# Sums of MLP weights: where GpSimd begins their transfers, and in what pieces

## The chip, the core and the metric

The kernel runs on one core of a Trainium2 chip. The core has a matrix engine (TensorE, PE in the profile, with its weight loads as PEld), a vector engine (VectorE, DVE), a scalar engine (ScalarE, ACT), a general engine (GpSimd, POOL) and a queue engine that only issues transfers (SyncE, SP). Sixteen DMA engines carry all transfers. Each engine takes its instructions in the order in which they were written into the program, and semaphores make it wait for the others. The metric is the device time of one execution in microseconds (us).

## The reference, cut to what matters

Two layers of a transformer run over 1024 latent tokens and 256 context tokens of width 1024, in 32-bit floats. Each layer computes a modulation from a conditioning vector, one input projection whose columns feed three mixers (latent attention, differential attention, a chunk mixer), an output projection, and a gated MLP with a convolution of three taps along the tokens.

```python
def conv_ffn(h, p):
    u = dwconv3(h @ p["ffn_wup"], p["ffn_convw"], p["ffn_convb"])
    gate, val = jnp.split(u, 2, axis=-1)
    return (jax.nn.silu(gate) * val) @ p["ffn_wdown"]

def layer(x, xc, mod, modc, rows, cols, p, layer_idx, need_ctx):
    sh1, sc1, g1, sh2, sc2, g2 = jnp.split(mod, 6, axis=-1)
    csh1, csc1, cg1, csh2, csc2, cg2 = jnp.split(modc, 6, axis=-1)
    y, yc = mixer(x * (1.0 + sc1) + sh1, xc * (1.0 + csc1) + csh1, rows, cols, p, layer_idx, need_ctx)
    x = layer_norm(DN_ALPHA * x + g1 * y, p["ln1_g"], p["ln1_b"])
    x = layer_norm(DN_ALPHA * x + g2 * conv_ffn(x * (1.0 + sc2) + sh2, p), p["ln2_g"], p["ln2_b"])
    ...
    return x, xc
```

The weights `ffn_wup` (1024 x 5632) and `ffn_wdown` (2816 x 1024) of each layer are what the change is about. The context tokens pass through the MLP in layer 0 only.

## The kernel before, in words

**The sums.** The two products of the MLP are computed with a scheme of Strassen's kind: a matrix is cut into two by two blocks, and seven block products replace eight. The scheme needs sums of weight blocks, such as block (1,0) plus block (1,1). The kernel has these sums made in DRAM by transfers alone: one transfer copies a block of weights into a scratch tensor, and a second one adds another block onto it on its way (an accumulation). The up weights of a layer have four such sums, kept in the tensor `ws`, and the down weights four more, kept in `db`. Two of the four are made from the inputs alone, the other two add a sum that is already made. All of these transfers are begun by POOL, in the function `sums` (the copy in line 592, the accumulation in line 593), and each sum is cut into chunks of 1408 KB: four chunks for a sum in `ws` and two for one in `db`. That makes 32 transfers for `ws` and 16 for `db` in each layer, 96 in all. `SUMROWS` and the function `flat` set the shape of a chunk: 176 rows of 2048 numbers, so 8 KB a row. A copy may join rows, and goes as 32 rows of 45 KB; an accumulation keeps rows of 8 KB.

**Where they are begun.** `sums` returns a list of steps, and `begin_sums(n)` takes the next n of them. Before the change the list for `ws` of layer 0 is made at the very start. In the input projection of each layer (`in_chunk`) one step is taken at every fourth tile. What is left is spread over the attention, between the pieces of the modulation, as fill (`program`). In the first part of the MLP (`ffn`, the "up" part) a new list is made, the `db` of this layer and, in layer 0, the `ws` of layer 1, and one or two steps are taken for each of 22 blocks of columns; what is left of it is begun in layer 1's input projection and attention.

**The order of the work.** The program is not written out in its final order. Each step is a task with the engines that may do it, an estimate of its time on each, the tasks that it depends on and a key. A planner (`Sched.run`) goes through time with these estimates and gives each engine the ready task with the smallest key, inside a window of 450 tasks. A sum's transfer is a task of 1.0 us on POOL with 120 added to its key and 40 us of delay after it, whatever its shape. The order that comes out is fixed: on the chip each engine follows its own list. So a step that takes longer than planned delays all that stands behind it on its engine.

**What else POOL does.** In the attention POOL joins the two maps of differential scores (lines 1237 and 1238, some 4.3 us for 1280 keys), which PE transposes one block of queries later (line 1262), and takes the low parts of weights (line 457). A block is one head and 256 queries, so layer 0 has 20 blocks and layer 1 has 16. In the MLP POOL makes combinations of blocks (line 1490).

**The readers of the sums.** `up_load` reads `ws`, and `down_load` reads `db`, both through SP; `sum_chunks` names the chunks that a read has to wait for. The MLP's up part stores its result in `da` (and `dc` for the context), from which the down part reads it again. Line 1671 is the scalar part of the convolution, and line 1650 the vector instruction that frees PE's accumulator for the next block. The input projection stores some of its results in `zd` (line 444 issues every transfer of SP).

Of the kernel before, what the change touches and what calls it, by code (L numbers as in the profile page):

```python
# [15 lines left out]
ALU = mybir.AluOpType  # L16
# [4 lines left out]
P = 128  # L21
# [9 lines left out]
NF = FF // P  # L31
NP = NF // 2
# [34 lines left out]
SIZES = [1280] * 17 + [1536] * 8 + [2560] * 8  # L67
LARGE = 512
UNIT = 64
SUMROWS = 176  # L70
SLACK = 150
AHEAD = 300

# [317 lines left out]
class Kern:  # L391
# [120 lines left out]
    def center(self, x, sums):  # L512

        nc = self.nc
        nm, ss, sq = self.st(), self.st(), self.C()
        self.task(dve_t(1), lambda e: nc.vector.tensor_scalar(nm.t, sums[0].t, sums[1].t, -1.0 / D, op0=ALU.add, op1=ALU.mult), sums, [nm])

        self.task(act_t(D, 0.19), lambda e: nc.scalar.activation(sq.t.bitcast(BF16), x[:, :D], AF.Square, bias=nm.t, accum_out=ss.t), [x, nm], [sq, ss])
        return nm, self.rsqrt1(lambda: ss.t, 1.0 / D, EPS, [ss])

    def norm(self, x, sums):

        nm, y = self.center(x, sums)
        b = self.st()
        self.task(dve_t(1), lambda e: self.nc.vector.tensor_tensor(out=b.t, in0=nm.t, in1=y.t, op=ALU.mult), [nm, y], [b])
        self.task(act_t(D, 0.18), lambda e: self.nc.scalar.activation(x[:, :D], x[:, :D], AF.Identity, scale=y.t, bias=b.t), [x, y, b], [x])
# [49 lines left out]

    def flat(self, x, c):

        return x.rearrange("n p c -> (n p c)").rearrange("(r c) -> r c", c=2048)[c * SUMROWS:(c + 1) * SUMROWS]

    def sums(self, l, which):

        src = self.i["wup" if which == "ws" else "w_down"]
        x = (self.ws if which == "ws" else self.db)[l]
        w = lambda a, b: (lambda: src[l, a, b])
        out = []

        def make(n, c, a, b, r=()):
            key = (which, l, n, c)
            put = lambda: self.flat(x[n], c)  # L590
            kw = dict(w=[key], key=MODKEY, late=40.0)
            out.append(lambda: self.s.add({"pool": 1.0}, lambda e: self.nc.gpsimd.dma_start(out=put(), in_=self.flat(a(), c)), (), **kw))
            out.append(lambda: self.s.add({"pool": 1.0}, lambda e: self.nc.gpsimd.dma_start(out=put(), in_=self.flat(b(), c), accum_op=ALU.add, max_dma_last_dim=8192), [*r, key], **kw))

        for c in range((NF if which == "ws" else NP) * P * 512 // (SUMROWS * 2048)):
            at = lambda n: (which, l, n, c)
            if which == "ws":
                make(0, c, w(1, 0), w(1, 1))
                make(2, c, w(1, 0), w(0, 0))
                make(1, c, w(0, 0), lambda: x[0], [at(0)])  # L600
                make(3, c, w(0, 1), lambda: x[1], [at(1)])
            else:
                make(0, c, w(0, 0), w(0, 1))
                make(1, c, w(0, 1), w(1, 1))
                make(2, c, w(1, 1), lambda: x[0], [at(0)])
                make(3, c, w(1, 0), lambda: x[2], [at(2)])
        return out
# [6 lines left out]

    def sum_chunks(self, name, l, n, f):
        a, b = f * P * 512, (f + 1) * P * 512 - 1
        m = SUMROWS * 2048
        return [(name, l, n, c) for c in range(a // m, b // m + 1)]


# [260 lines left out]
    def in_chunk(self, l, name, tabs):  # L881
        i = self.i
        if (l, name) not in self.inw:
            self.chunk_weights(l, name)
        wk, wb = self.inw.pop((l, name))
        if name == "dk":
            tabs["d"] = td = self.C(F32, (P, 8, 2, 32))
            self.dma(lambda: td.t, lambda: i["dtab"], 4 * P * 512, w=[td])
        elif name == "kv":
            tabs["k"] = tk = self.S(F32, (P, 8, 2, 64))  # L890
            self.dma(lambda: tk.t, lambda: i["ktab"], 4 * P * 1024, w=[tk])
            self.kvT = [(self.S(F32R), self.S(F32R)) for _ in range(2)]
            self.krs = self.S(F32R)
        elif name == "q":
            self.qlT = {p: (self.S(F32R, (P, 3, 256)), self.S(F32R, (P, 3, 256))) for p in range(NT // 2)}
        held = []
        tiles = range(0 if l == 0 or name in ("kv", "dk", "dv") else 2, NT)
        if name == "z":
            tiles = (8, 9, 0, 1) if l == 0 else (6, 7, 8, 9, 2, 3, 4, 5)
        for n, t in enumerate(tiles):  # L900
            if name != "z" and n % 4 == 1:
                self.begin_sums(1)
            r = self.in_tile(l, name, t, wk, wb, tabs)
            if r is not None:
                held.append(r)
                if len(held) == 2:
                    self.transpose_lat(name, t - 1, held)
                    held = []
# [881 lines left out]
    def ffn(self, l):  # L1790
        nc, i = self.nc, self.i
# [3 lines left out]
        self.dn_raw, self.dn_ops = [], []  # L1795
        order = self.up_order(l)
        last = order[-1][1]
        assert not self.due
        self.due = self.sums(l, "db") + (self.sums(1, "ws") if l == 0 else [])
        done = 0  # L1800
        for x in order:
            if len(x) == 2:
                self.emit_rest(x)
                continue
            done += x[2] != 1
            self.up_operands(l, done - 1 + UP_LOOK)
            f = x[0]
            self.up_slot(l, *x)
            if f >= 2 and (x[1] == "22" or l == 0 and f % 2 and x[1] == "S2"):
                self.begin_sums(1)  # L1810
            if f == NF - 1 and x[1] == "S3":
                self.down_load(l, 2)
            if f == NF - 1 and x[1] == "22":
                self.down_prep(l, 1)
            if x[1] == last and f % 2:
                self.store_pair(l, f // 2, self.blocks[f - 1:f + 1])
                self.blocks[f - 1] = self.blocks[f] = None
# [5 lines left out]
        for n, pr in enumerate(DOWN):  # L1823
# [14 lines left out]
            if n in (2, 4):  # L1838
                for t, u in pairs:
                    x = u if n == 2 else t  # L1840
# [10 lines left out]
            for m, (t, u) in enumerate(pairs):  # L1851
# [3 lines left out]
                a, b = acc[t], acc[u]  # L1855
# [49 lines left out]
    def program(self):  # L1905
        self.setup()
        self.first_hT()
        self.due = self.sums(0, "ws")
        for l in range(DEPTH):
            self.in_proj(l)  # L1910
            self.att_setup(l)
            ada = [(0, n) for n in range(8, 24)] + [(1, n) for n in range(8)] if l == 0 else [(1, n) for n in range(8, 24)]
            ada = [lambda a=a: self.mod_piece(*a, MODKEY) for a in ada]
            m, d = len(ada), len(self.due)
            fill = []
            for j, a in enumerate(ada):
                fill += [lambda: self.begin_sums(1)] * ((j + 1) * d // m - j * d // m) + [a]
            self.attention(l, fill)
            self.out_tiles(l, NT, True)
            self.ffn(l)  # L1920
# [103 lines left out]
```

## Time and profile before

| what | value |
|---|---|
| runs shown, median (lowest to highest) | 3523.48 us (3515.53 to 3527.67) |
| the profiled execution's own time | 3522.21 us |
| its span, first to last instruction | 3520.4 us |
| PE busy, share of the span | 3210.6 us, 91% |
| DVE busy | 2586.0 us, 73% |
| ACT busy | 1652.2 us, 47% |
| POOL busy | 1045.3 us, 30% |
| DMA queue of SP, share of 16 engines | 34.1% (386.22 MB) |
| DMA queue of POOL, share of 16 engines | 15.9% (138.42 MB) |

The span is 1.8 us shorter than the execution's own time. In the program's order the first layer's input projection lies at about 130 to 345 us, its attention at 345 to 870, the up part of its MLP from about 980 to 1665 and the down part to 2080; the second layer's input projection lies at 2080 to 2180, its attention at 2180 to 2670, its up part at about 2800 to 3265 and the down part to the end. A share over the whole span mixes these stages, so the prediction reads each of them by itself. "Issue" as a releaser means that the profile shows nothing that the engine waited for.

### The profile page before, as it was taken

To read this page: it belongs to the slowest core of one execution; us is meant where nothing else is said; L and a number is where in the kernel's file an instruction comes from. 1 tells how busy PE (TensorE), PEld (TensorE's weight loads), DVE (VectorE), ACT (ScalarE), POOL (GpSimd) and SP (SyncE) were. 2 spreads that over 40 slices of the span, in tenths; PEclk is the share of its full clock that TensorE was granted. 3 is DMA by queue.
4 is the path that set the end of the run, shared out by engine and by line. 5 is a ranking of instruction groups with operands and counts; after the bars stand their busy time and mean duration, and the time that the engine had idled before them with its cause. 6 is when DMAs were issued, how large, how long until landed. Compare 5 with 4: busy or idle time off the path is not lost. (4 is left out here: it accounts for less than half of the span.)

```text
span 3520.4 us, 53639 instructions
## 1 busy us (share of the span) xinstructions
PE 3210.6 (91%) x18953; PEld 2801.2 (80%) x18953; DVE 2586.0 (73%) x6262; ACT 1652.2 (47%) x2931; POOL 1045.3 (30%) x678
## 2 busy tenths in 40 slices
PE   7799999998988889989998899999998889999997
PEld 5798888787977777777886799888888867788775
DVE  7456988988777566657569737889898776666687
ACT  5024666565344344434435404566663445454543
POOL 3101555553122111213034301454434232212143
PEclk9899999999999999999999999999998999999998
DMA  8823444443345666664765743132313556653672
GB/s 324 206 65 100 116 120 131 120 106 104 111 145 168 191 176 181 191 173 147 225 217 188 213 130 78 49 77 82 89 53 121 163 157 200 201 163 132 222 263 102
DMA packets 274839, 528.07 MB, mean 150 GB/s; under 512 B 67465, under 2 KB 119177, under 8 KB 264585
## 3 DMA queue, kind: packets, MB, share of 16 engines
q1 hardware_dynamic: 263048, 386.22, 34.1%
q0 software_dynamic: 11520, 138.42, 15.9%
q8 instruction: 149, 2.44, 0.3%
q14 instruction: 122, 0.99, 0.1%
HBM read 444.25 MB, written 218.69 MB: 188 GB/s over the span
## 5 line engine op out<-in xcount | busy, mean ns | idle before, releaser
L447 PE MATMUL t<-region 128*128 128x256 f32 (+4 forms) x15631 | 2876.0, 342 | 233.4 <-DVE region L457 69.7
L447 PEld LDWEIGHTS t<-region 128*128 128x128 f32 x15631 | 2458.0, 194 | 584.9 <-DVE region L457 82.6
L457 DVE TENSOR_TENSOR region<-region 128x512 fp32r<-128x512 f32 (+6 forms) x867 | 765.2, 907 | 267.8 <-ACT region L460 225.0
L460 ACT ACTIVATE region<-t 128x512 fp32r<-128x512 f32 (+4 forms) x935 | 452.6, 511 | 717.1 <-PE t L447 326.0
L460 ACT ACTIVATE region<-region 128x512 fp32r<-128x512 f32 (+4 forms) x944 | 591.2, 662 | 384.8 <-PE t L447 131.9
L457 POOL TENSOR_TENSOR region<-region 128x512 fp32r<-128x512 f32 (+5 forms) x289 | 403.9, 1408 | 1123.2 <-ACT region L460 804.6
L1490 POOL TENSOR_TENSOR region<-region 128x512 f32<-128x512 f32 (+2 forms) x107 | 212.0, 1984 | 911.3 <-ACT region L460 355.2
L1673 DVE SCALAR_TENSOR_TENSOR region<-region,conv 128x1023 f32<-128x1023 f32 x176 | 233.4, 1327 | 165.6 <-ACT region L1671 165.3
L1198 ACT ACTIVATE region<-region,q 128x1280 f32<-128x1280 f32 (+1 forms) x216 | 273.5, 1267 | 165.2 <-DVE q L1197 148.7
L1193 DVE TENSOR_SCALAR_CACHE_REDUCE region<-t 128x512 f32<-128x512 f32 (+1 forms) x600 | 333.6, 586 | 9.4 <-PE t L447 8.0
L457 DVE TENSOR_TENSOR region<-t,region 128x512 fp32r<-128x512 f32 (+1 forms) x529 | 297.8, 598 | 46.4 <-ACT region L460 41.6
L1262 PE MATMUL t<-ident,region 128*128 128x128 f32 x1312 | 186.1, 285 | 19.9 <-DVE region L1193 5.0
L1238 POOL TENSOR_TENSOR region<-region 128x1280 f32<-128x1280 f32 (+1 forms) x69 | 188.4, 2731 | 5.8
L1262 PEld LDWEIGHTS t<-ident,region 128*128 128x128 f32 x1312 | 154.9, 147 | 27.6 <-DVE region L1193 8.2
L1671 ACT ACTIVATE region<-region,conv 128x1024 f32<-128x1024 f32 x88 | 109.2, 1241 | 128.2 <-DVE region L1654 56.7
L1237 POOL TENSOR_SCALAR region<-region,q 128x1280 f32<-128x1280 f32 (+1 forms) x69 | 87.4, 1267 | 205.6 <-DVE q L1232 128.2
L447 PE MATMUL t<-region,s 128*4 128x256 f32 x768 | 118.2, 291 | 17.2 <-ACT region L460 10.8
L1490 DVE TENSOR_TENSOR region<-region 128x512 f32<-128x512 f32 (+2 forms) x150 | 113.3, 760 | 18.4 <-POOL region L1490 15.3
L1018 DVE TENSOR_TENSOR region<-t,region 128x256 f32<-128x256 f32 x32 | 13.6, 424 | 126.5 <-PE t L447 69.6
L447 PEld LDWEIGHTS t<-region,s 128*4 128x4 f32 x768 | 64.8, 87 | 46.4 <-ACT region L460 11.3
L548 POOL TENSOR_TENSOR region<-region 128x1024 f32<-128x1024 f32 x26 | 72.8, 2815 | 93.3 <-DMA region<-n 65.6
L1688 ACT ACTIVATE region<-region 128x1024 f32<-128x1024 f32 x66 | 53.4, 839 | 63.9 <-DVE region L1673 63.9
(137 smaller groups left out, 1849.5 us busy)
## 6 DMA issues: line engine op xcount, KB each, us to landing
ws<-in_wup POOLq DMA_DIRECT2D x48, 1408.0 KB, 9.8
region<-ws SPq DMA_DIRECT2D x176, 256.0 KB, 3.7
region<-in_ada_w SPq DMA_DIRECT2D x160, 256.0 KB, 3.5
region<-in_wup SPq DMA_DIRECT2D x154, 256.0 KB, 3.0
da<-region SPq DMA_DIRECT2D x154, 256.0 KB, 3.7
region<-da SPq DMA_DIRECT2D x154, 256.0 KB, 4.0
db<-in_w_down POOLq DMA_DIRECT2D x24, 1408.0 KB, 8.5
ws<-ws POOLq DMA_DIRECT2D x16, 1408.0 KB, 14.3
```

What stands on the lines that cost most here:

```text
L447: self.nc.tensor.matmul(ps, a, b, start=start, stop=stop, skip_group_check=again)
L457: eng.tensor_tensor(out=out, in0=full, in1=hi.bitcast(F32), op=ALU.subtract)
L460: self.nc.scalar.activation(out, in_, AF.Copy, **kw)
L548: self.task(engs or pool_t(D), lambda e, row=row, op=op: self.vec[e].tensor_tensor(out=x[:, :D], in0=x[:, :D], in1=row.t, op=op), [x, row] ...
L1193: self.task(dve_t(b - a), lambda e: nc.vector.tensor_scalar(p[:, a:b], ps[:, :b - a], -scale, None, op0=ALU.mult, op1=ALU.min, accum_out=n ...
L1198: self.task(act_t(nk, 0.19), lambda e: nc.scalar.activation(p[:, :nk], p[:, :nk], AF.Exp, bias=m.t, scale=-1.0, accum_out=s.t), [p, m], [p ...
L1237: nc.gpsimd.tensor_scalar(p2[:, :nk], p2[:, :nk], cc.t, 0.0, op0=ALU.mult, op1=ALU.add)
L1238: nc.gpsimd.tensor_tensor(out=p1[:, :nk], in0=p1[:, :nk], in1=p2[:, :nk], op=ALU.add)
L1262: nc.tensor.transpose(ps[:, u, j * P:(j + 1) * P], B[key][j][:, (kt + u) * P:(kt + u + 1) * P], self.ident)
L1490: self.task(either(n), lambda e: self.vec[e].tensor_tensor(out=o(), in0=a(), in1=b(), op=op), r, w, **kw)
L1671: self.task(act_t(n, 0.15), lambda e: nc.scalar.activation(t.t, u(0, n), AF.Identity, scale=c[:, 1:2], bias=c[:, 3:4]), r + ["conv"], [t])
L1673: self.task(dve_t(n - 1, extra=0.06), lambda e, d=d: nc.vector.scalar_tensor_tensor(t[:, 1 - d:n - d], u(d, n - 1 + d), c[:, 2 * d:2 * d + ...
```

## The change

All 48 transfers of a layer's sums are now taken as fill in the attention of that layer, spread evenly between the pieces of its modulation. Neither the input projection nor the MLP begins any. The rows of a chunk become 704 rows of 512 numbers, 2 KB a row, for copies and accumulations alike; a chunk still has 1408 KB and there are still 96 transfers. The space in which POOL keeps what it has put out for the DMA engines (`dynamic_dma_scratch_size`) grows from 1024 to 2048 bytes.

```diff
-SUMROWS = 176
+SUMROWS = 704
...
     def flat(self, x, c):
-        return x.rearrange("n p c -> (n p c)").rearrange("(r c) -> r c", c=2048)[c * SUMROWS:(c + 1) * SUMROWS]
+        return x.rearrange("n p c -> (n p) c")[c * SUMROWS:(c + 1) * SUMROWS]
...
-            out.append(lambda: self.s.add({"pool": 1.0}, lambda e: self.nc.gpsimd.dma_start(out=put(), in_=self.flat(a(), c)), (), **kw))
-            out.append(lambda: self.s.add({"pool": 1.0}, lambda e: self.nc.gpsimd.dma_start(out=put(), in_=self.flat(b(), c), accum_op=ALU.add, max_dma_last_dim=8192), [*r, key], **kw))
+            out.append(lambda: self.s.add({"pool": 1.0}, lambda e: self.nc.gpsimd.dma_start(out=put(), in_=self.flat(a(), c), max_dma_last_dim=2048), (), **kw))
+            out.append(lambda: self.s.add({"pool": 1.0}, lambda e: self.nc.gpsimd.dma_start(out=put(), in_=self.flat(b(), c), accum_op=ALU.add, max_dma_last_dim=2048), [*r, key], **kw))
...
-        for n, t in enumerate(tiles):
-            if name != "z" and n % 4 == 1:
-                self.begin_sums(1)
+        for t in tiles:
...
-        assert not self.due
-        self.due = self.sums(l, "db") + (self.sums(1, "ws") if l == 0 else [])
...
-            if f >= 2 and (x[1] == "22" or l == 0 and f % 2 and x[1] == "S2"):
-                self.begin_sums(1)
...
-        self.due = self.sums(0, "ws")
         for l in range(DEPTH):
             self.in_proj(l)
             self.att_setup(l)
...
+            self.due = self.sums(l, "ws") + self.sums(l, "db")
             m, d = len(ada), len(self.due)
...
-    nc = _bacc.Bacc("TRN2", target_bir_lowering=False, num_devices=1, dynamic_dma_scratch_size=1024)
+    nc = _bacc.Bacc("TRN2", target_bir_lowering=False, num_devices=1, dynamic_dma_scratch_size=2048)
```

The planner places the rest anew, so the order changes on every engine. From line 900 on the changed program's line numbers are smaller by two, and from line 1800 on by up to six. The places on which the prediction rests are on POOL. The first is POOL's list in the first input projection, before the change; a row with `x2` stands for two equal instructions, and 176x2048 is the shape of an accumulation:

```order
L592 DMA ws<-in_wup 32x11264
L593 DMA ws<-in_wup 176x2048 x2
L948 TENSOR_TENSOR region<-region 128x256
L593 DMA ws<-in_wup 176x2048
L457 TENSOR_TENSOR region<-region 128x1280
L1027 TENSOR_TENSOR region<-region 128x256
L593 DMA ws<-in_wup 176x2048
L593 DMA ws<-ws 176x2048 x2
L592 DMA ws<-in_wup 32x11264
L593 DMA ws<-ws 176x2048
L457 TENSOR_TENSOR region<-region 128x1152
L593 DMA ws<-ws 176x2048
```

The same place in the changed program, with the first transfers at its end:

```order
L457 TENSOR_TENSOR region<-region 128x1280
L457 TENSOR_TENSOR region<-region 128x768
L937 TENSOR_TENSOR region<-region 128x256 x2
L946 TENSOR_TENSOR region<-region 128x256
L457 TENSOR_TENSOR region<-region 128x1280
L1025 TENSOR_TENSOR region<-region 128x256
L457 TENSOR_TENSOR region<-region 128x1152
L592 DMA ws<-in_wup 704x512 x2
L457 TENSOR_TENSOR region<-region 128x2x2x32
L457 TENSOR_TENSOR region<-region 128x256
```

The ten copies and accumulations of the first list have gone from among the tiles of the projection, and the first sums begin behind its last weight (128x1152).

The second place is in the attention of the first layer, about two thirds through it. Before, one transfer stands between several blocks' joins (L1237, L1238):

```order
L457 TENSOR_TENSOR region<-region 128x512 x6
L1237 TENSOR_SCALAR region<-region,q 128x1280
L1238 TENSOR_TENSOR region<-region 128x1280
L1237 TENSOR_SCALAR region<-region,q 128x1280
L1238 TENSOR_TENSOR region<-region 128x1280
L593 DMA ws<-in_wup 176x2048
L457 TENSOR_TENSOR region<-region 128x512 x3
L1237 TENSOR_SCALAR region<-region,q 128x1280
L1238 TENSOR_TENSOR region<-region 128x1280
L1237 TENSOR_SCALAR region<-region,q 128x1280
L1238 TENSOR_TENSOR region<-region 128x1280
L592 DMA ws<-in_wup 32x11264
```

In the changed program (where the joins are L1235 and L1236):

```order
L1235 TENSOR_SCALAR region<-region,q 128x1280
L1236 TENSOR_TENSOR region<-region 128x1280
L1235 TENSOR_SCALAR region<-region,q 128x1280
L1236 TENSOR_TENSOR region<-region 128x1280
L593 DMA ws<-ws 704x512
L593 DMA ws<-in_wup 704x512 x2
L457 TENSOR_TENSOR region<-region 128x10x64
L592 DMA ws<-in_wup 704x512
L457 TENSOR_TENSOR region<-region 128x512
L592 DMA db<-in_w_down 704x512
L457 TENSOR_TENSOR region<-region 128x512 x2
```

Five transfers of 704 rows stand there with two small steps between them.

The third place is the up part of the first layer's MLP, before:

```order
L1490 TENSOR_TENSOR region<-region 128x512 x3
L593 DMA db<-db 176x2048
L1490 TENSOR_TENSOR region<-region 128x1024
L592 DMA db<-in_w_down 32x11264
L593 DMA db<-in_w_down 176x2048
L1490 TENSOR_TENSOR region<-region 128x1024
L1490 TENSOR_TENSOR region<-region 128x512 x3
L592 DMA db<-in_w_down 32x11264
L593 DMA db<-in_w_down 176x2048
L1490 TENSOR_TENSOR region<-region 128x1024
L1490 TENSOR_TENSOR region<-region 128x512
L592 DMA db<-in_w_down 32x11264
```

And in the changed program, where the combinations are line 1488:

```order
L1488 TENSOR_TENSOR region<-region 128x512
L1488 TENSOR_TENSOR region<-region 128x1024
L1488 TENSOR_TENSOR region<-region 128x512
L1488 TENSOR_TENSOR region<-region 128x1024
L1488 TENSOR_TENSOR region<-region 128x512 x3
L1488 TENSOR_TENSOR region<-region 128x1024
L1488 TENSOR_TENSOR region<-region 128x512
L1488 TENSOR_TENSOR region<-region 128x1024
```

Every transfer has gone from POOL's list there.

## Rows read from the trace of the kernel before

**Rows 1.** Busy time by stretch: stretch, length, busy time per engine, granted clock, DMA share, GB/s.

```profile
core 0: us, PE busy (x) PEld busy (x) DVE busy (x) ACT busy (x) POOL busy (x), PEclk, DMA share, GB/s
130.00:345.00 215.00, 191.23 (x1390) 185.67 (x1389) 100.47 (x472) 56.05 (x147) 15.15 (x17) 0.93 0.45 116
345.00:870.00 525.00, 485.35 (x3402) 432.99 (x3402) 476.27 (x1428) 331.96 (x653) 267.52 (x182) 0.96 0.41 114
1060.00:1570.00 510.00, 451.18 (x2231) 377.71 (x2230) 316.80 (x395) 205.76 (x334) 100.38 (x70) 0.95 0.64 182
1570.00:1665.00 95.00, 89.48 (x467) 75.48 (x466) 64.21 (x76) 43.72 (x70) 22.03 (x12) 1.00 0.51 149
1920.00:2050.00 130.00, 115.97 (x652) 100.66 (x652) 90.84 (x306) 45.23 (x71) 38.37 (x38) 0.95 0.75 218
2180.00:2670.00 490.00, 450.35 (x3136) 402.11 (x3135) 435.49 (x1246) 301.94 (x564) 219.95 (x131) 0.96 0.29 80
2800.00:3100.00 300.00, 274.99 (x1199) 222.77 (x1198) 203.41 (x228) 146.64 (x228) 74.38 (x43) 0.96 0.63 187
3100.00:3265.00 165.00, 160.49 (x694) 129.11 (x692) 111.33 (x127) 84.24 (x125) 33.51 (x14) 1.00 0.46 148
```

**Rows 2.** Timeline of PE, 150 to 180 us: start, length, work [idle before, releaser].

```profile
172.50 7.73 PE L447 MATMUL t<-region 128*128 128x256 f32 x50 [19.43 <-DVE region L1024]
```

**Rows 3.** Timeline of DVE, 165 to 173 us.

```profile
171.41 0.43 DVE L1018 TENSOR_TENSOR region<-t,region 128x256 f32<-128x256 f32 x1 [39.83 <-DMA zd<-region]
```

**Rows 4.** Waits of PE, 1055 to 1665 us: who for whom: total, times, longest.

```profile
PE t L447 <- DVE region L1650: 36.3, 8, 7.7
```

**Rows 5.** Waits of ACT, 1055 to 1665 us.

```profile
ACT region L1671 <- DMA da<-region: 48.7, 8, 11.6
```

**Rows 6.** DMA issues, 1055 to 1665 us: number, KB each, median us to landing.

```profile
da<-region SPq DMA_DIRECT2D x72, 256.0 KB, 10.7
ws<-in_wup POOLq DMA_DIRECT2D x11, 1408.0 KB, 8.2
db<-in_w_down POOLq DMA_DIRECT2D x8, 1408.0 KB, 9.9
db<-db POOLq DMA_DIRECT2D x4, 1408.0 KB, 13.0
...
ws<-ws POOLq DMA_DIRECT2D x3, 1408.0 KB, 14.4
```

**Rows 7.** DMA issues, 2800 to 3265 us.

```profile
da<-region SPq DMA_DIRECT2D x72, 256.0 KB, 2.3
```

**Rows 8.** Timeline of POOL, 110 to 150 us.

```profile
110.56 1.90 POOL L593 DMA_DIRECT2D ws<-in_wup  x2
...
125.39 0.88 POOL L593 DMA_DIRECT2D ws<-in_wup  x1 [6.67 <-issue]
...
133.65 0.87 POOL L593 DMA_DIRECT2D ws<-in_wup  x1 [3.73 <-issue]
141.18 0.88 POOL L593 DMA_DIRECT2D ws<-ws  x1 [6.66 <-issue]
149.83 0.86 POOL L593 DMA_DIRECT2D ws<-ws  x1 [7.76 <-issue]
```

**Rows 9.** Instructions on tensor ws: ns of one, min/median/max, first and last start.

```profile
L592 POOL DMA_DIRECT2D ws<-in_wup x32: 491/552/852, 46.3 to 2433.1; - x32
L593 POOL DMA_DIRECT2D ws<-in_wup x16: 857/905/1314, 110.6 to 2185.1; - x16
```

**Rows 10.** DMA queue of POOL on the page: packets, MB, share of 16 engines.

```profile
q0 software_dynamic: 11520, 138.42, 15.9%
```

**Rows 11.** DMA issues, 345 to 870 us.

```profile
ws<-in_wup POOLq DMA_DIRECT2D x10, 1408.0 KB, 7.5
ws<-ws POOLq DMA_DIRECT2D x4, 1408.0 KB, 10.3
```

**Rows 12.** Waits of PE, 345 to 870 us.

```profile
PE t L1262 <- POOL region L1238: 0.8, 1, 0.8
```

More of the change, by code (lines that the diff above doesn't have):

```diff
@@ L591, in make @@
             kw = dict(w=[key], key=MODKEY, late=40.0)
-            out.append(lambda: self.s.add({"pool": 1.0}, lambda e: self.nc.gpsimd.dma_start(out=put(), in_=self.flat(a(), c)), (), **kw))
-            out.append(lambda: self.s.add({"pool": 1.0}, lambda e: self.nc.gpsimd.dma_start(out=put(), in_=self.flat(b(), c), accum_op=ALU.add, max_dma_last_dim=8192), [*r, key], **kw))
-        for c in range((NF if which == "ws" else NP) * P * 512 // (SUMROWS * 2048)):
+            out.append(lambda: self.s.add({"pool": 1.0}, lambda e: self.nc.gpsimd.dma_start(out=put(), in_=self.flat(a(), c), max_dma_last_dim=2048), (), **kw))
+            out.append(lambda: self.s.add({"pool": 1.0}, lambda e: self.nc.gpsimd.dma_start(out=put(), in_=self.flat(b(), c), accum_op=ALU.add, max_dma_last_dim=2048), [*r, key], **kw))
+        for c in range((NF if which == "ws" else NP) * P * 512 // (SUMROWS * 512)):
             at = lambda n: (which, l, n, c)
@@ L616, in sum_chunks @@
         a, b = f * P * 512, (f + 1) * P * 512 - 1
-        m = SUMROWS * 2048
+        m = SUMROWS * 512
         return [(name, l, n, c) for c in range(a // m, b // m + 1)]
```

## The prediction

> **What bounds the kernel now.** I read the busy time by stretch first [rows 1]. Column by column the reader should look at PE busy against the length of the stretch, then at DVE, then at POOL. In the attention of layer 0 (345 to 870 us) PE works 485.35 of 525 us and DVE 476.27: two engines at 92% and 91%, POOL at 51%. Attention of layer 1 (2180 to 2670) is the same picture, 450.35 and 435.49 of 490, POOL 219.95. The feed-forward of layer 0 is looser: PE idles 58.8 us of the 510 from 1060 to 1570, in which the sums are moved, and only 5.5 of the 95 just behind them. In layer 1 it idles 25.0 of 300 while its sums run and 4.5 of 165 when they are over. PE's time and its gaps set the end; the question is what the moved transfers put into those gaps and what they take out.
>
> Next I read who is waited for at the gaps. The largest single gap of the whole program is 19.43 us, ended by DVE at 172.50 [rows 2]; DVE itself had stood 39.83 us for a store to zd [rows 3]. That is the first input projection, where POOL puts out accumulation after accumulation. In the first feed-forward PE waits 36.3 us in eight places for the line that starts a new block's convolution [rows 4]; ACT, which feeds it, stands 48.7 us for stores to da [rows 5], and such a store takes 10.7 us there [rows 6] against 2.3 us in layer 1 [rows 7]. Both stretches pay for the sums by stores that land late.
>
> **What goes away.** (a) First input projection: no sum runs beside it any more, so the gap of 19.43 goes. What is late next there is the remainder of 23.8 us idle, 4.4 us, and I leave that: -19 us, bounds 0 and -24. (b) Feed-forward of layer 0: 26 transfers (11 + 8 + 4 + 3 in [rows 6]) leave. Without them PE idles at 2.7% (4.5 of 165) to 5.8% (5.5 of 95) [rows 1], which is 14 to 30 us of 510 in place of 58.8: -29 to -45, I take -37. Next in line there is the copy from PSUM that PE also waits for, inside the 14 to 30 us left. (c) Feed-forward of layer 1: 25.0 idle becomes 8 to 17, I take -12. (d) End of layer 0's down projection (1920 to 2050): 14 us idle with sums of the next layer beside it; no row ties its waits to them, so the bounds are 0 and -14, and I take -5, nearer to nothing since its neighbour rows do not name a DMA. Sum of (a) to (d): -73 us, between -37 (c at -8, a and d at nothing, b at -29) and -100.
>
> The granted clock stands at 0.95 in the stretch with gaps and at 1.00 in the two without [rows 1]. If (b) and (c) ran at 1.00 they would save another 5% of 451 + 275 us of PE work, up to 36 us; the attention, now at 0.96, would lose in the same way if it gets gaps. I let the two cancel and keep 36 us of it for the range.
>
> **What is added to the attentions.** All 96 transfers now stand in the attentions, 48 in each, against 14 in the first before (10 + 4 in [rows 11]). Three costs.
>
> First, issuing. A copy of 32 rows holds POOL 0.55 us, an accumulation of 176 rows 0.905 [rows 9]: 2.45 ns for a row more, so 704 rows give 0.55 + 672 x 0.00245 = 2.2 us (an estimate; no change would be 0.55 and 0.9, in proportion to the rows 3.6). 48 x 2.2 is 106 us of POOL per attention. Alone that is hidden in POOL's 258 us of idle time in the first and 270 in the second.
>
> The Trainium skill's page "SBUF — State Buffer" ("A bandwidth-pool intuition that's wrong" and the trap above it) says that GpSimd can't write a transfer's descriptors while DVE holds the shared port, so that a 0.62 us transfer becomes 3.1 us beside a DVE copy. In these rows DVE is 91% busy and an issue reaches at most 0.85 and 1.31 us against medians of 0.55 and 0.905 [rows 9]. By the page's ratio of five the 2.2 us would be 11; by the rows it would be 3.2 at most. I go by the rows.
>
> Second, room for transfers that are begun and not ended. At 110.56 POOL puts out two accumulations; the third starts at 125.39 after 6.67 us in which nothing that the profile shows is missing, and the next at 133.65, 141.18 and 149.83, one every 7.5 to 8.7 us [rows 8]. I read this as two accumulations of 176 rows in flight and no room for a third, with POOL standing at the head of its queue until one has landed. The change makes four times the rows in each and doubles the scratch space: room for at least 2 and under 3 times 176 becomes room for 704 to 1055 rows, so one accumulation. Every sum that follows one closely now waits for its landing, and behind it waits POOL's arithmetic: the joins of the differential scores (line 1238) and the splits of weights. In POOL's order most transfers stand in bursts: in the first attention 34 of 48, in the second 31, have at most three instructions between them and the one before. Walking down the order with an accumulation holding the room for 8 us, 22 wait in each. One wait is 10.3 us from issue to landing [rows 11] less 2.2 for the issue, 8.1, behind an accumulation, and 7.5 - 2.2 = 5.3 in the row that mixes copies in; I take 7. That is 154 us of standing per attention. POOL's account for the first: 267.5 - 14 x 0.73 + 106 + 154 = 517 of 525 us; for the second 220 + 106 + 154 = 480 of 490. POOL becomes a third full engine.
>
> What of it reaches PE? Today PE waits 0.8 us for a join in the first attention [rows 12], so the joins come early, by up to a block of 26 us (20 blocks in 525 us). Single waits of 7 us hide in that. The bursts don't: in the first attention four of them (five to seven transfers each) hold POOL for 24 to 30 us. I charge PE half of it, 15 us each, and 3 us for each of four smaller ones: 72 us. In the second the transfers come in about fourteen groups of two to four, 7 to 15 us of standing each, mostly inside the lead; I charge 2 us each, 28. Together 100 us; from below nothing (all hidden), from above the whole standing, 308.
>
> Third, the DMA engines. The sums took 15.9% of the span on all engines [rows 10], 560 us for 96, 5.8 each, so 48 x 5.8 = 280 us of a 500 us attention, on top of 0.41 - 14 x 5.8 / 525 = 0.25: about 0.8 of the engines' time. I cost this at nothing beside the second item, because the first attention, with 14 sums and a share of 0.41, idles PE 7.6%, and the second, with a share of 0.29, idles it 8.1% [rows 1].
>
> Sum: 3522.2 (profiled execution, span 3520.4 plus 1.8 around it; the median of the three runs is 3523.5) - 73 + 100 = 3549, so 3550.
>
> **Rivals.** (R1) POOL's idle time takes it all. POOL is idle half of each attention, PE waits for it 0.8 us, and pieces of 2 KB hold up a store or load for a quarter of the time. Then only the gains are left, 3522 - 73 = 3449, to 3415 with the clock. Against it stands the account of 517 in 525 us. The Trainium skill's page "DMA: Bandwidth & Descriptors" ("Queues, rings and completion order") speaks for it: an engine turns between queues only when a whole packet is done. That agrees with the stores of 10.7 against 2.3 us, and by it smaller pieces let others through sooner.
>
> (R2) The price goes with the transfer and not with POOL: in (b) and (c) a sum costs PE 37 us / 26 = 1.4 us wherever it runs beside loads. 78 more sums in the attentions (34 + 44) then cost 109 us: 3522 - 73 + 109 = 3558. It would show as PE and ACT waiting for loads and not for POOL. Against it: the equal idle shares of the two attentions.
>
> (R3) It moves nothing: gains and costs meet within 0.3% (11 us, about what a measurement of this kernel can tell from no change), 3512 to 3533. That needs an attention price of 62 to 84 us, inside the bounds of the second item.
>
> **Chances.** Forecast, 3550, with a range of its own from 3533 to 3640: 0.46. R2 0.11. R1, with everything down to 3512: 0.31. R3 0.12. So faster 0.31, no change 0.12, slower 0.57. The middle of R1 lies at 3450 and a price of twice mine (200 us) gives 3650; the range 3450 to 3640 leaves out about 2 in 10. The forecast turns to faster where the price in the attentions falls under 62 us, that is when under a fifth of POOL's standing reaches PE.
>
> **What would show it.** Right: issues of 2 us and more in POOL's rows; idle time of POOL without a named releaser before transfers, 100 us or more in each attention; POOL named by PE, or by DVE and ACT one step before, for tens of us there; the gap at 172 us gone; stores to da near 2.3 us in both feed-forwards and PE's wait for the convolution line in the first down to a few us. Wrong: attentions of 525 and 490 us or shorter with POOL standing (then its lead is longer than I charge), no standing at all (then the room is not what rows 8 show), or a first feed-forward as long as before without sums in it (then the late stores had another cause).

## The result and the profile after

The changed kernel takes 3583.26 us (median of four runs, 3576.51 to 3588.61) against 3524.36 us for the kernel before in the same job: a ratio of 1.017, 95% interval 1.0145 to 1.0195. It is slower by 59 us. The forecast was 3550, 28 us above the profiled execution of before; the profiled execution of after is 3576.51 us, 54 above it. The sign and the range hold; the rise is twice the one forecast.

Where the 54 us lie is read by stage. The marks are instructions that both kernels have: the first and the last exponential of an attention, the first run of line 1650 in an up part (the vector instruction that empties PE's accumulator), the start of the last convolution step. In layer 1 of before, and of the experiments with its places, the attention is counted from 1.2 us ahead of its first exponential. Lines behind the two deleted places stand two lower in the changed kernel (before's 1650 is 1648, 1671 is 1669, 1238 is 1236).

| stage, us | before | after | difference |
|---|---|---|---|
| start to first exponential of layer 0 | 347.2 | 323.3 | -23.9 |
| attention 0 | 509.7 | 611.3 | +101.6 |
| its output projection | 188.5 | 186.5 | -2.0 |
| up part of layer 0 | 618.7 | 544.0 | -74.7 |
| down part of layer 0, input projection 1 | 554.5 | 533.7 | -20.8 |
| attention 1 | 448.0 | 516.0 | +68.0 |
| its output projection | 173.2 | 185.2 | +12.0 |
| up part of layer 1 | 424.1 | 416.9 | -7.2 |
| down part of layer 1 | 256.5 | 257.8 | +1.3 |

Five stages give back 129 us, and the attentions with the projection behind the second cost 182. Busy time by stretch, cut at the same marks, first of before (stretch, length, busy time of each engine with its number of instructions, granted clock, DMA share, GB/s), then of after:

```profile
347.20:856.90 509.70, 473.11 (x3317) 421.38 (x3316) 462.19 (x1357) 325.92 (x640) 262.04 (x177) 0.97 0.42 116
1045.40:1664.10 618.70, 553.48 (x2773) 464.51 (x2773) 392.79 (x485) 255.72 (x412) 126.67 (x86) 0.96 0.61 175
2218.60:2666.60 448.00, 415.45 (x2918) 371.68 (x2917) 410.99 (x1192) 283.62 (x523) 212.31 (x125) 0.97 0.28 80
```

```profile
323.30:934.60 611.30, 492.75 (x3342) 435.32 (x3340) 458.43 (x1361) 329.53 (x647) 285.91 (x203) 0.89 0.64 161
1121.10:1665.10 544.00, 532.51 (x2774) 453.71 (x2773) 400.17 (x474) 255.39 (x412) 127.56 (x71) 0.99 0.41 129
2198.80:2714.80 516.00, 439.08 (x2920) 386.62 (x2921) 415.35 (x1185) 286.01 (x523) 247.76 (x164) 0.92 0.69 168
```

Length less PE busy is PE's idle time. In the up part it falls from 65.2 to 11.5 us, and the same number of matmuls takes 21 us less at a granted clock of 0.99 for 0.96 (a mean over its two levels: 1.00 is 2.4 GHz, 0.5 is 1.2 GHz). In attention 0 the idle time grows from 36.6 to 118.6 us, in attention 1 from 32.6 to 76.9, the granted clock falls to 0.89 and 0.92, and PE's work there is longer by 20 and 24 us (25 and 2 matmuls more are in the stretches).

The relief shows as foreseen. The gap at 172.50 [rows 2] is gone; the timeline of PE over it:

```profile
149.74 30.52 PE L447 MATMUL t<-region 128*128 128x256 f32 x258
```

The stores to da [rows 6] land in 3.7 us in the up part of layer 0, and no wait of PE for the convolution line [rows 4] is left there. DMA issues of after in 1121 to 1665 us, then all waits of PE in that stretch:

```profile
da<-region SPq DMA_DIRECT2D x72, 256.0 KB, 3.7
```

```profile
PE t L447 <- ACT region L460: 7.6, 9, 2.4
PE t L447 <- DVE region L457: 2.2, 2, 1.5
PE t L447 <- POOL region L457: 1.7, 2, 1.0
```

The price shows too. The transfers of the sums, tensor ws (instructions with ns of one, min/median/max, then POOL's idle time before them), and the same idle line for tensor db:

```profile
L592 POOL DMA_DIRECT2D ws<-in_wup x32: 674/712/862, 220.8 to 2413.0; - x32
L593 POOL DMA_DIRECT2D ws<-in_wup x16: 1112/1137/1178, 263.2 to 2441.6; - x16
L593 POOL DMA_DIRECT2D ws<-ws x16: 1093/1142/1311, 311.4 to 2538.7; - x16
...
  issue: 186.2, 22
```

```profile
  issue: 86.0, 9
```

POOL stands 272 us in 31 waits with no releaser that the profile shows, 8.8 us each; 132 us of it lie in the first attention and 106 in the second. One chain shows how this gets to PE. POOL's timeline around 600 us, then PE's at 607 us:

```profile
580.90 1.17 POOL L593 DMA_DIRECT2D ws<-ws  x1
593.82 1.14 POOL L593 DMA_DIRECT2D ws<-in_wup  x1 [11.75 <-issue]
604.58 1.11 POOL L593 DMA_DIRECT2D ws<-in_wup  x1 [9.63 <-issue]
605.29 1.95 POOL L457 TENSOR_TENSOR region<-region 128x640 fp32r<-128x640 f32 x1
```

```profile
607.29 0.75 PE L1125 MATMUL t<-identr,region 128*128 128x128 f32 x4 [18.70 <-POOL region L457]
```

Between 582 and 605 us POOL does nothing but begin two transfers. The split of a weight (line 457) stands behind them in POOL's order and runs only then; PE has waited 18.70 us for it. Over the whole attention 0, waits of PE, then of POOL (who for whom, total, times, longest):

```profile
PE t L447 <- POOL region L457: 33.2, 5, 15.0
PE t L1125 <- POOL region L457: 24.4, 2, 18.7
...
PE t L1176 <- POOL region L457: 10.0, 1, 10.0
```

```profile
POOL ws L592 <- issue: 46.7, 6, 11.3
...
POOL ws L593 <- issue: 33.7, 4, 11.7
POOL db L593 <- issue: 32.8, 3, 11.9
POOL db L592 <- issue: 19.1, 3, 10.1
```

So 67.6 us of PE's waits name POOL for line 457. The join, 0.8 us before [rows 12], is 0.2. In the second attention PE's waits name POOL for 8.5 us only, again for line 457; what the standing costs there is read from experiment 3.

### The profile page after: what moved, and what is told of

It reads as the page before. It is cut to its first block, busy times and chain, and to the rows that moved or that the text cites. A ratio compares the mean times of both kernels' runs of the same rounds, so it can differ in the third digit from the quotient of the medians.

```text
span 3574.7 us, 53654 instructions
## 1 busy us (share of the span) xinstructions
PE 3225.6 (90%) x18953; PEld 2813.3 (79%) x18953; DVE 2599.5 (73%) x6242; ACT 1656.5 (46%) x2933; POOL 1088.8 (30%) x696
## 5 line engine op out<-in xcount | busy, mean ns | idle before, releaser
L457 DVE TENSOR_TENSOR region<-region 128x512 fp32r<-128x512 f32 (+7 forms) x862 | 752.9, 898 | 174.9 <-ACT region L460 144.5
L457 POOL TENSOR_TENSOR region<-region 128x512 fp32r<-128x512 f32 (+6 forms) x294 | 413.2, 1433 | 923.3 <-ACT region L460 512.8
L1488 POOL TENSOR_TENSOR region<-region 128x512 f32<-128x512 f32 (+2 forms) x121 | 239.0, 1978 | 835.3 <-DVE region L1671 360.7
L1236 POOL TENSOR_TENSOR region<-region 128x1280 f32<-128x1280 f32 (+1 forms) x69 | 187.4, 2716 | 5.8
L1260 PEld LDWEIGHTS t<-ident,region 128*128 128x128 f32 x1312 | 156.8, 148 | 30.5 <-DVE region L1191 13.5
L1235 POOL TENSOR_SCALAR region<-region,q 128x1280 f32<-128x1280 f32 (+1 forms) x69 | 88.6, 1284 | 153.9 <-DVE q L1230 71.6
L447 PEld LDWEIGHTS t<-region,s 128*4 128x4 f32 x768 | 65.2, 88 | 78.7 <-POOL region L457 30.4
L1686 ACT ACTIVATE region<-region 128x1024 f32<-128x1024 f32 x66 | 53.4, 840 | 69.2 <-DVE region L1671 69.2
```

The lines of the kernel that those rows point to most:

```text
L447: self.nc.tensor.matmul(ps, a, b, start=start, stop=stop, skip_group_check=again)
L457: eng.tensor_tensor(out=out, in0=full, in1=hi.bitcast(F32), op=ALU.subtract)
L1235: nc.gpsimd.tensor_scalar(p2[:, :nk], p2[:, :nk], cc.t, 0.0, op0=ALU.mult, op1=ALU.add)
L1236: nc.gpsimd.tensor_tensor(out=p1[:, :nk], in0=p1[:, :nk], in1=p2[:, :nk], op=ALU.add)
L1260: nc.tensor.transpose(ps[:, u, j * P:(j + 1) * P], B[key][j][:, (kt + u) * P:(kt + u + 1) * P], self.ident)
L1488: self.task(either(n), lambda e: self.vec[e].tensor_tensor(out=o(), in0=a(), in1=b(), op=op), r, w, **kw)
```

## The experiments

Two theories stood after the result. **Room**: POOL's standing is the price, and with room or small needs for room the attentions are as before. **Engines**: the sums in the attention hold the DMA engines from other loads, whatever POOL does; the standing is at most a part. A third question came up with the second kernel: the change alters two things, places and sizes, and they may pull against each other.

**1. The changed places, the pieces of before** (8 KB accumulations, whole copies, scratch 1024).

```
-SUMROWS = 704
+SUMROWS = 176
...
-    dynamic_dma_scratch_size=2048
+    dynamic_dma_scratch_size=1024
```

> The change's places (all sums in the attentions) with the pieces of before: accumulations of 176 rows of 8 KB, copies of 32 rows, scratch 1024. The order on every engine is that of the changed kernel. Theory (POOL stands because one accumulation fills the room, and that is what the attentions pay): with room for two accumulations again POOL's standing before sums falls from 272 us to under 90, the attentions come from 611 and 516 us to about 530 to 550 and 455 to 475, and the whole to 3440 to 3480. Rival (a sum costs PE some 1.4 us beside loads wherever it is begun, through the DMA engines): attentions stay at 600 and 510 or get longer with the coarser pieces, the whole 3570 to 3620.

Measured: 3580.03 us, ratio 1.0164 (1.0143 to 1.0185), as slow as the changed kernel. A miss for the room theory: POOL stands 0.2 us in the whole program, yet the attentions take 584.3 and 538.3 us, 165 more than before with the same pieces and the same scratch. In attention 0, waits of ACT and DVE, then a DMA issue:

```profile
ACT region L460 <- DMA region<-in_ada_w: 69.9, 14, 24.7
```

```profile
DVE region L1170 <- DMA region<-zd: 42.3, 5, 14.3
```

```profile
region<-in_cst SPq DMA_DIRECT2D x16, 128.0 KB, 13.1
```

ACT stands for loads of the modulation weights (9.5 us in before), DVE for z, and the rotation table in_cst lands after 13.1 us, where before had 3.0. So the sums cost much even when POOL does not stand, and what ACT and DVE wait for then are loads of SP's queue. In the changed kernel ACT's wait is 24.1 and in_cst takes 5.9, but pieces and standing both differ from here. In experiment 3, which keeps the small pieces and takes most of the standing away, the two are 21.9 and 9.8: the step in ACT's wait goes with the large pieces, and part of that in in_cst with the standing.

**2. The places of before, the pieces of the change** (2 KB, scratch 2048).

```
-SUMROWS = 176
+SUMROWS = 704
...
-    dynamic_dma_scratch_size=1024
+    dynamic_dma_scratch_size=2048
```

> The places of before with the change's pieces (704 rows of 2 KB, scratch 2048), order on every engine as before. Theory (room): standing only where transfers follow each other closely, in the first input projection, whose gap of 19 us stays or grows to 40; in the first feed-forward POOL has slack of tens of us, so the stage stays at 606 us or falls if the finer pieces let stores of da through (landing under 6 us in place of 10.7, then about 570). The whole 3490 to 3545. Rival (pieces are what makes the attentions of the changed kernel slow only together with the place, and stores are late because of the bytes moved): the first feed-forward stays at 600 to 610 and da stores at 10 us, the whole 3515 to 3540.

Measured: 3431.11 us, ratio 0.9742 (0.9724 to 0.9759): 93 us faster than before and 152 faster than the changed kernel, beyond what was expected. Attentions 513.1 and 447.7, up part of layer 0 553.9 us. POOL's idle lines for the tensors ws and db, then waits of ACT and of PE in that up part (1036 to 1590 us):

```profile
  issue: 157.6, 20
```

```profile
  issue: 64.4, 9
```

```profile
ACT region L460 <- DMA region<-in_wup: 27.0, 18, 3.3
ACT region L1671 <- DMA da<-region: 26.3, 5, 11.4
```

```profile
PE t L447 <- ACT region L460: 10.6, 8, 3.5
...
PE t L447 <- DVE region L1650: 2.5, 4, 0.8
```

POOL stands 222 us here too, 64 of them in this up part, and PE hardly notices: its waits name POOL for 2.0 us there, and the wait for the convolution line is 2.5 us where it was 36.3 [rows 4]. The size of the pieces (with the scratch that goes with it) is a large gain; the places are a loss with either size.

**3. The changed kernel with room for two** (scratch 4096 for 2048, nothing else).

> The changed kernel with one number changed: scratch 4096 in place of 2048. Theory (room): two accumulations of 704 rows in flight, so POOL's standing falls from 272 us to 60 to 140 and the attentions by half of their price, to about 560 and 480; the whole 3480 to 3530. Rival (DMA engines or the issue itself): no difference from the changed kernel, 3575 to 3590.

Measured: 3498.35 us, ratio 0.9934 (0.9913 to 0.9956), inside what room expected. Its stretches of the attentions, and the idle lines of ws and db:

```profile
323.90:879.50 555.60, 486.83 (x3342) 430.46 (x3341) 460.81 (x1362) 330.10 (x648) 287.27 (x203) 0.93 0.69 177
...
2150.40:2640.20 489.80, 430.47 (x2920) 379.26 (x2921) 411.87 (x1185) 285.50 (x523) 248.19 (x164) 0.95 0.71 177
```

```profile
  issue: 17.6, 3
```

```profile
  issue: 18.2, 4
```

The standing falls from 272 to 36 us and the attentions by 55.7 and 26.2 us: 82 us for 236 us of standing, 0.35 for one. But 555.6 and 489.8 are still 42 us each above the attentions of experiment 2, which has nearly the same pieces with 14 transfers in the first and 4 in the second. Room is about one half of the price in the attentions.

**4. Large pieces with more room** (experiment 1 with scratch 2048).

```
-    dynamic_dma_scratch_size=1024
+    dynamic_dma_scratch_size=2048
```

> The change's places, pieces of 8 KB and scratch 2048: room for four or more accumulations of 176 rows. Theory (room): next to no standing (under 30 us), attentions of 515 to 535 and 450 to 465 us, the whole 3420 to 3460, faster than both kernels. Rival (DMA engines): as x1_att_8k within 10 us, and not faster than before.

Measured: 3580.40 us, ratio 1.0164 (1.0145 to 1.0184), attentions 584.6 and 543.4: a miss for room, and no change against experiment 1. With 8 KB pieces room is not what binds.

**5. The fastest kernel with room for two** (experiment 2 with scratch 4096).

> The sums at the places of the kernel before, in pieces of 2 KB, with a scratch of 4096 instead of 2048. With 2048 GpSimd stood 157.6 us in 20 waits before these transfers, and the kernel took 3431.11 us. Theory: standing costs only where TensorE soon wants a weight that GpSimd splits, as in the attention; at these places GpSimd has time. Then the standing goes and the time falls by 0 to 15 us, to 3415 to 3431. Rival: standing costs everywhere at the rate seen in the attention (272 us stood, some 85 us paid, 0.31 us for each): 3431 - 157.6 x 0.31 = 3382, so 3375 to 3395.

Measured: 3450.19 us, ratio 0.979 (0.9771 to 0.981). Both sides missed (the 157.6 us of the expectation are those before transfers of ws alone; with db it is 222). With 32 us of standing left, none of it in the up part of layer 0, it is 19 us slower than experiment 2, and the two intervals lie apart. The start gains 11.5 us, but the up part of layer 0 goes from 553.9 to 584.1. There, waits of ACT:

```profile
ACT region L1671 <- DMA da<-region: 53.8, 7, 10.8
ACT region L460 <- DMA region<-in_wup: 36.5, 17, 4.7
```

PE's waits behind them, for lines 460 and 1650, are 24.6 and 6.1 us (10.6 and 2.5 in experiment 2). The same transfers, begun as soon as POOL comes to them, keep da's stores and in_wup's loads longer than when POOL has to stand between them. Little room acts as a throttle on POOL's queue; that is worth something where POOL has time (here) and costs where PE wants its splits (the attention).

**6 and 7. Which pieces matter.** Places of before; in 6 only the copies are small, in 7 only the accumulations (scratch 2048 in both).

```
-in_=self.flat(a(), c)), (), **kw)
+in_=self.flat(a(), c), max_dma_last_dim=2048), (), **kw)
```

> The kernel before, with its places; only the plain copies of each sum go in small pieces, the accumulations stay at 8 KB. Theory: it is the large pieces of the copies that delay the small loads and stores on the engines (with all in small pieces the stores of da land in 3.7 us instead of 10.7, and the kernel gains 93 us). Then most of the 93 us comes with this edit: 3431 to 3465, and the stores of da near 4 us. Rival: the accumulations' 8 KB pieces delay the others: 3500 to 3525 here, the stores of da at 8 us or more.

> The counterpart: places of the kernel before, the accumulations in pieces of 2 KB (scratch 2048), the copies in their large pieces as before. Theory (the copies' pieces delay the others): 3490 to 3525, stores of da at 8 us or more. Rival (the accumulations' pieces do): 3431 to 3465, stores of da near 4 us. If both share the delay, this one and its counterpart each lie near 3478.

Measured for 6: 3509.29 us, ratio 0.9957 (0.9938 to 0.9976). For 7: 3469.40 us (median of three executions), ratio 0.9843 (0.982 to 0.9865). The same kernel was run once more for its rows:

> The same kernel as x7_spread_accum (places of the kernel before, accumulations in pieces of 2 KB, copies in large pieces, scratch 2048), whose profile was no use. Its three other executions were 3460.64 to 3470.12 us; the same is expected here, 3458 to 3478. If the accumulations' pieces are what delays the others, the wait of ScalarE's L460 for region<-in_wup, 72.7 us before, 30.9 us with both in 2 KB and 85.9 us with only the copies small, is under 55 us here; if GpSimd's standing alone spreads the transfers, it is still near 72 us and the gain comes from fewer engines' time held at once.

Measured: 3467.28 us, ratio 0.9853 (0.9831 to 0.9875). My theory that the copies' large pieces do the harm is a miss: they are worth 13 us, the accumulations' 54, and both together 93. Waits of ACT in the up part of layer 0, of before, of 6, then of 7 run again:

```profile
ACT region L460 <- DMA region<-in_wup: 66.3, 14, 10.2
```

```profile
ACT region L460 <- DMA region<-in_wup: 65.5, 13, 10.6
ACT region L1671 <- DMA da<-region: 48.1, 7, 11.1
```

```profile
ACT region L1671 <- DMA da<-region: 57.4, 8, 11.0
ACT region L460 <- DMA region<-in_wup: 38.1, 14, 5.9
```

In the kernel before the wait for da was 48.7 [rows 5]. Small copies change neither. Small accumulations take 28 us off the loads of in_wup (in the whole program 72.7 becomes 54.7, just under the 55 that was set as the limit). In this up part POOL stands before no sum in 6, 7 and 5, so this is the pieces and not the standing. The stores to da stay late, and fall only in experiment 2, where the standing spaces the transfers as well. The gains add up in the same way: 13 and 54 are near the 72 of experiment 5, which has both and little standing, and some 20 more come in experiment 2.

**8. Fewer bytes, the same order.** Experiment 3 with each accumulation cut to 88 of its 704 rows; it leaves out most of the sums, so only its time is of use.

```
-out=put(), in_=self.flat(b(), c), accum_op=ALU.add, max_dma_last_dim=2048)
+out=put()[:88], in_=self.flat(b(), c)[:88], accum_op=ALU.add, max_dma_last_dim=2048)
```

> All sums in the attention, pieces of 2 KB, scratch 4096, as in the kernel that took 3498.35 us; the copies are whole, but each accumulation takes only the first 88 of its 704 rows, so most of the sums is left out. The number of GpSimd's instructions, their order and their places stay. In that kernel the attentions took 555.6 and 489.8 us, against 513.1 and 447.7 with the sums spread, 84 us together. Theory: this rest goes with the bytes that the accumulations move on the DMA engines; at least half of it goes: 3440 to 3465. Rival: it comes from the places of the transfers in GpSimd's order and the joins and weight splits behind them, whatever they move: 3485 to 3500.

Measured: 3435.07 us, ratio 0.9755 (0.9732 to 0.9779), 63 us less than experiment 3 and 5 below the theory's range. Attentions 521.3 and 468.7: of the 84 us that were left, 55 go. POOL's queue in attention 0 of experiment 3, then of this one (packets, MB, share of 16 engines), and here the wait of ACT for the modulation weights, 21.9 us there:

```profile
q0 software_dynamic: 22480, 59.12, 45.1%
```

```profile
q0 software_dynamic: 10384, 32.62, 21.1%
```

```profile
ACT region L460 <- DMA region<-in_ada_w: 0.9, 2, 0.7
```

The number and order of POOL's instructions are those of experiment 3, so these 55 us go with what the accumulations move. They are not all the engines': the 36 us of standing that were left go too, and PE's longest waits in attention 0 that name POOL were in experiment 3

```profile
PE t L1176 <- POOL region L457: 8.0, 1, 8.0
PE t L1125 <- POOL region L457: 7.7, 1, 7.7
```

and 3.5 us more; here 0.2 are left for line 457. That is 19 of the 55; the other 36 are an estimate of what the sharing of the engines cost. The last 29 us were not settled; the order that the planner made anew is one candidate.

One piece of the price is neither room nor bytes. In the output projection behind the second attention PE waits once for a load of the tensor n, here as experiment 3 shows it:

```profile
2743.97 1.08 PE L1415 MATMUL t<-ident,region 128*128 128x128 f32 x4 [13.44 <-DMA region<-n]
```

The same wait of 13.4 to 13.5 us stands in every kernel with the changed places, whatever the pieces, the scratch or the bytes, and in none with the places of before. POOL's queue takes at most 0.3% of the engines there in after and in experiment 3. It goes with the new order.

## Why the prediction was right or wrong

**What goes away, -73: 129 measured.** (a) was -19, measured -23.9: PE idles 21.0 us less there, the gap of 19.43 and little else, and has 2.9 us less work. (b) was -37, measured -74.7: of the gains this term was mis-sized most. I left 14 to 30 us of idle in the up part, read from stretches of before without sums; 11.5 are left, 54 less, and at the clock of 0.99 PE's work takes another 21 us less, which I had booked apart. (c) -12, measured -7.2. (d) -5, measured -20.8 with the next input projection in it, which had no term: I chose the low end for lack of a row.

**The clock, let cancel.** -21 us in the up part of layer 0 against +20 and +24 in the attentions, where I had said that it would be lost if gaps came. Over these three stretches that leaves +23, inside the 36 kept for the range.

**Issuing, 2.2 us each, hidden.** Measured 0.71 and 1.14 us; the line through 32 rows of a copy and 176 of an accumulation was too steep. Little hangs on it, as POOL had 258 and 270 us of idle time for either. The ratio of five that the Trainium skill's "SBUF — State Buffer" ("A bandwidth-pool intuition that's wrong") gives for a transfer beside a DVE copy isn't seen: DVE is busy 458 of 611 us, and no transfer of the sums took POOL over 1.31 us to begin. Whether DVE held the shared port in that time no row shows.

**Room in flight, 308 us of standing and 100 us of PE: right in mechanism and near in size.** Measured 272 us in 31 waits of 8.8, 238 of them in the attentions, instead of 44 of 7. What it costs is shown by experiment 3, which takes away 236 of it: 56 us in the first attention and 26 in the second, against my 72 and 28. Wrong was who carries it to PE: I named the joins; it is the splits of weights, which I had listed behind them.

**The DMA engines, costed at nothing: this step failed.** The prediction worked out a share of about 0.8 (measured 0.64 and 0.69) and set its cost to nothing because two attentions with shares of 0.41 and 0.29 idle alike [rows 1]. Two points at low shares say nothing of a third at 0.7. Experiment 1, in which POOL stands 0.2 us, has attentions 165 us longer than before, with ACT waiting for loads. With small pieces and room for two the sums in the attentions still cost 84 us against experiment 2; experiment 8 puts 55 of them to what the accumulations move, 36 by estimate to the engines alone, and 29 stay open. R2 had this price, 109 us, and its sign, late loads at ACT. R2 and the second item were put as rivals; experiments 1 and 3 show that both prices are there. Their sum, 100 + 109, is near the 182 measured, but that proves nothing: the price for each transfer changes with the pieces.

**The new order, without a term.** The output projection behind the second attention takes 185.2 us in after and 187.4 in experiment 3, against 173.2 in before and 164.6 in experiment 2. The wait of 13.5 us for n is most of it.

So the 26 us beyond the forecast are two errors that nearly met: 56 us too little relief, 82 us too little cost. That the time lies inside the range is in this sense luck.

**R1** failed on POOL's standing, but its remark on small pieces is right for the accumulations. The rule of the Trainium skill's "DMA: Bandwidth & Descriptors" ("Queues, rings and completion order"), that an engine turns to another queue only at a packet's end, agrees with ACT's wait for in_wup, 66.3 to 38.1 us with 2 KB accumulations. With small copies the wait is 65.5, although the copies' packets were the longest of before: 45,056 bytes and 1.9 us in the trace, against 8,192 bytes and 0.63 us for the accumulations' (medians). Why only the accumulations' pieces count stays open. The prediction never priced the pieces in the places of before: that is the 93 us of experiment 2, and the change throws it away by its places.

## What to carry to other kernels

Split a change of places and sizes into its halves and price each: here the sizes gain 93 us, and the places lose 56 with large pieces and 152 with small ones. Before bulk transfers move under the tightest stage, add up two prices and not the larger of them: what stands behind the issuing engine's head of queue, and whose loads share the DMA engines at the new share. The kernel to keep is experiment 2, the places of before with 2 KB pieces and a scratch of 2048.

## What the runs showed of the hardware

- Room for begun transfers can be too large: doubling it gained 85 us where POOL's later work was due (3583.26 to 3498.35) and lost 19 where it was not (3431.11 to 3450.19).
- An issue's time rises little with the rows: 704 took 0.71 us as a copy, where 32 took 0.55, and 1.14 as an accumulation, where 176 took 0.905 [rows 9].
- Small pieces cost a little more of the engines' time. POOL's queue on the page of after (packets, MB, share of 16 engines):

```profile
q0 software_dynamic: 52224, 138.42, 17.0%
```

Experiment 1, in the same places with large pieces, has 11520 packets and 15.0%; in the places of before it is 15.9% with large pieces [rows 10] and 17.8% with small ones (experiment 2). Four and a half times the packets for the same bytes add about 2 points of share in either places, and spread as before they shorten what others wait for. In the trace of after an accumulation's packets have 2,048 bytes, as its rows do; a copy's have 4,096, though its rows have 2,048.

- An accumulation holds the engines longer than a copy of the same bytes: in the trace of before the packets of each kind carry 69.2 MB, and their times, shared over 16 engines, are 364 us for the accumulations and 195 for the copies.
